# The small parts of 48 MLP weight chunks from an adding DMA, and 24 rounded parts from a casting DMA

## The chip, the cores and the metric

The kernel runs on one core of a Trainium2 chip. The metric is device time in microseconds. On the core, TensorE (PE in the profile) multiplies, VectorE (DVE) and ScalarE (ACT) work on whole tiles, GpSimd (POOL) does little here, and SyncE (SP) issues the weight loads. SP and POOL issue DMAs, which 16 DMA engines carry out for both.

## The reference: what is computed

One decoder layer on 256 tokens of width 2048 in float32: differential attention and a causal convolution module side by side, merged by gates, a projection, then an MLP of width 8192.

```python
m = jax.nn.sigmoid(zga) * attn_out + jax.nn.sigmoid(zgc) * conv_out
h = h + rms_norm(m @ w_out[l], post_mix_gain[l], NORM_EPS)
u = rms_norm(h, pre_ff_gain[l], NORM_EPS)
f = jnp.square(jax.nn.relu(u @ w_ff1[l])) @ w_ff2[l]
h = h + rms_norm(f, post_ff_gain[l], NORM_EPS)
```

All matrix products together read about 285 MB of weights once.

## The kernel before

**Weights as two parts.** TensorE multiplies in float32r, a rounded float32. To keep the precision, each weight w is split into wh, w rounded to float32r, and wl = w - wh; the activations likewise. Each product is then three: wh with the large and the small part of the activation, and wl with the large part.

**Chunks.** All weights come in 272 chunks of 128 x 2048 float32 (1 MiB), in the order in which they are multiplied (`order`, lines 66 to 77). The last 128 are the MLP's: four quarters q, each with 16 chunks of w_f1 (`ct` 0 to 15) and then 16 of w_f2 (four blocks `n` of four `kc`). A chunk of w_f1 is multiplied by `ws_k` (line 168 with wh, 512 columns; line 171 with wl, 256 columns; 16 of each), one of w_f2 by `as_part` (lines 194, 195 and 196, of which 195 reads wl; 24 matmuls of 512 columns in all).

**From the load to the matmul.** `fill` keeps up to three chunks alive (WBUFS = 3): there are three buffers each of raw, wh and wl. For a chunk, SP loads raw (line 97), ScalarE writes wh (`split_hi`, line 103), VectorE writes wl = raw - wh (`split_lo`, line 109). wh and wl of a chunk are free when TensorE has done with the chunk three before; raw is free when the subtraction three before has read it. `take` hands the chunk to TensorE and `done` lets the next fill begin.

**Order.** A scheduler that simulates the program sets the order of each engine's instructions, except for pinned ones at the beginning of the kernel and of the MLP; each engine then works through its own list in that order and waits at its head. In the MLP ScalarE and VectorE also take the results out of PSUM: lines 185, 186, 638, 640, 153 and 154 for w_f1 (sum, scale, squared ReLU, split of the activation), 648 or 650 for w_f2. POOL issues four DMAs in the whole kernel and none in the MLP but the first of its stretch (line 627, the last gain).

Of the kernel before, what the change touches and what calls it, by code (L numbers as in the profile page):

```python
# [13 lines left out]
AF = mybir.ActivationFunctionType  # L14
ALU = mybir.AluOpType
# [7 lines left out]
KT = D // P  # L23
# [5 lines left out]
CHUNK = 2048  # L29
NB = D // 512  # L30
# [22 lines left out]
def tile_layer(ctx, tc, x, vecs, lams, rope_t, subln, b_conv, post_mix, post_ff,  # L53
               w_q, w_k, w_v, w_cv, w_cg, w_ga, w_gc, w_co, w_o, w_f1, w_f2, out):
    nc = tc.nc
# [9 lines left out]
    order = []  # L65
# [6 lines left out]
    for w in (w_ga, w_gc, w_co, w_o):  # L72
        order += [w[n, kc] for n in range(NB) for kc in range(4)]
    n_mix = len(order)
    for q in range(NQ):
        order += [w_f1[q * KT + ct] for ct in range(KT)]
        order += [w_f2[n, q * 4 + kc] for n in range(NB) for kc in range(4)]
    queue = []
    state = {"next": 0, "live": 0}

# [2 lines left out]
    def load(pieces):  # L83
        i = state["next"]
        state["next"] += 1
        state["live"] += 1
        chunk = (rawp.tile([P, CHUNK], F32, name="raw"), whp.tile([P, CHUNK], F32R, name="wh"),
                 wlp.tile([P, CHUNK], F32R, name="wl"))
        for j in range(pieces):
            load_part(chunk, i, j, pieces)  # L90
        queue.append(chunk[1:])
        return chunk

    def load_part(chunk, i, j, pieces, pinned=False):
        w = CHUNK // pieces
        sl = slice(j * w, (j + 1) * w)
        a = nc.sync.dma_start(chunk[0][:, sl], order[i][:, sl])
        if pinned:
            pin(a)

    def split_hi(chunk, a, b, pinned=False):
        raw, wh, wl = chunk
        i = nc.scalar.copy(wh[:, a:b], raw[:, a:b])  # L103
        if pinned:
            pin(i)

    def split_lo(chunk, a, b, eng=None, pinned=False):
        raw, wh, wl = chunk
        i = (eng or nc.vector).tensor_sub(wl[:, a:b], raw[:, a:b], wh[:, a:b].bitcast(F32))  # L109
        if pinned:  # L110
            pin(i)

    def fill():
        while state["live"] < WBUFS and state["next"] < len(order):
            pieces = 4 if state["next"] in (n_mix, n_mix + 1, n_mix + 3) else 1
            chunk = load(pieces)
            w = CHUNK // pieces
            for j in range(pieces):
                split_hi(chunk, j * w, (j + 1) * w)
                split_lo(chunk, j * w, (j + 1) * w)  # L120

    def take():
        if not queue:
            fill()
        return queue.pop(0)

    def done(refill=True):
        state["live"] -= 1
        if refill:
            fill()  # L130
# [384 lines left out]
    for j in range(8):  # L515
# [3 lines left out]
        for i in range(2):  # L519
            ct = 2 * j + i  # L520
# [44 lines left out]
    for n in range(NB):  # L565
        ps = as_block(ma, apart=(n == NB - 1))
        ns = slice(n * 512, (n + 1) * 512)
        with tc.high_priority(offset=CHAIN if n == NB - 1 else 0):
            for t in range(NT):
                sq = fin2.tile([P, 512], F32, name="fsq")  # L570
                nc.scalar.activation(sq, ps[t], AF.Square, accum_out=yss[:, t, n:n + 1])
                if n == NB - 1:
                    nc.scalar.activation(r1[:, t:t + 1], yss[:, t, n:n + 1], AF.Sqrt, bias=ypre[:, t:t + 1],
                                         scale=1.0 / D)
# [57 lines left out]
    for q in range(NQ):  # L632
# [9 lines left out]
        for n in range(NB):  # L642
            ps = as_block(ga, stagger=(q == NQ - 1 and n == NB - 1), apart=(q == NQ - 1 and n == NB - 1))
            ns = slice(n * 512, (n + 1) * 512)
            for t in range(NT):
# [5 lines left out]
                if q == NQ - 1:  # L651
                    last = n == NB - 1
                    with tc.high_priority(offset=CHAIN if last else 0):
                        sq = fin2.tile([P, 512], F32, name="fsq")
                        nc.scalar.activation(sq, dst, AF.Square, accum_out=fss[:, t, n:n + 1])
                        if last:
                            nc.scalar.activation(r3[:, t:t + 1], fss[:, t, n:n + 1], AF.Sqrt, bias=fpre[:, t:t + 1],
                                                 scale=1.0 / D)
# [75 lines left out]
```

## Time and profile before

| | before |
|---|---|
| time, median of 2 runs | 1568.25 us (1568.21 to 1568.29) |
| span of the profiled execution | 1566.2 us |
| TensorE busy | 1548.6 us, 99% |
| VectorE busy | 1105.2 us, 71% |
| ScalarE busy | 710.6 us, 45% |
| weight load, 1 MiB, issue to landing (median) | 4.8 us |
| mean data rate over the span | 190 GB/s |

The runs lie 2.0 us above the span, which runs from the first to the last instruction. Busy shares are averages over the whole kernel; the change is in the MLP alone, which begins after 840 us. A matmul's busy time overlaps with that of the next, so the pace of TensorE is read from the starts.

### The profile page before, as it was taken

Reading aid. Unit: us, or ns where it says so; the run is one execution under the profiler, and the core shown is the slowest. Engines: PE = TensorE matmul, PEld = TensorE weight load, DVE = VectorE, ACT = ScalarE, POOL = GpSimd, SP = SyncE. Lnnn points to the kernel's source line nnn. Section 1 sums busy time; section 2 is a strip of 40 time slices with the busy share of each in tenths; the row PEclk is TensorE's granted clock in tenths of the full one; section 3 lists DMA queues with packets and bytes.
Section 4 is the critical chain, followed back from the end, with each engine's and each line's share of the span. In section 5 each row is a group of like instructions: output and inputs, shape, how many; then the busy total and the mean of one; then the engine's idle time right before and its main releaser. Section 6 shows DMA issues by size and latency. Waiting matters only on the chain.

```text
span 1566.2 us, 19217 instructions
## 1 busy us (share of the span) xinstructions
PE 1548.6 (99%) x7870; PEld 1316.3 (84%) x7870; DVE 1105.2 (71%) x1391; ACT 710.6 (45%) x749; POOL 15.8 (1%) x36
## 2 busy tenths in 40 slices
PE   8999999999999999999999999999999999999997
PEld 7888888888888888888887888888888888888886
DVE  5999999999999977856546765456644665456654
ACT  5444454646454546633435543344433443334442
POOL 3000000000000000000000000000000000000000
PEclk8999999999999999999999999999999999999999
DMA  6655555544555555555754655555555555555552
GB/s 226 231 189 190 191 191 184 184 174 177 173 177 179 198 188 188 209 190 184 266 192 143 233 192 192 188 188 189 188 190 192 186 186 191 200 193 182 188 199 83
DMA packets 45863, 296.85 MB, mean 190 GB/s; under 512 B 5072, under 2 KB 5200, under 8 KB 11216
## 3 DMA queue, kind: packets, MB, share of 16 engines
q1 hardware_dynamic: 45072, 290.39, 52.4%
q0 software_dynamic: 704, 5.24, 0.9%
q8 instruction: 61, 1.00, 0.2%
q14 instruction: 26, 0.21, 0.0%
HBM read 293.52 MB, written 2.10 MB: 189 GB/s over the span
## 4 chain that ended last, share of the span: by engine, by line
PE 98%; DVE 1%; DMA 1%; ACT 0%; SPq 0%; issue 0%; DVEq 0%; ACTq 0%
PE ps L168 30%; PE ps L196 16%; PE ps L194 16%; PE ps L195 16%; PE ps L171 15%; PE po L454 1%; DMA x_sb<-in_x_dram 1%; PE s L426 0%; PE aux L234 0%; PE aux L194 0%; PE aux L195 0%; PE aux L196 0%; DVE y_sb L669 0%; PE s L425 0%; PE aux L547 0%; SPq L260 0%
## 5 line engine op out<-in xcount | busy, mean ns | idle before, releaser
L109 DVE TENSOR_TENSOR wl<-raw,wh 128x2048 fp32r<-128x2048 f32 (+2 forms) x286 | 620.3, 2171 | 395.2 <-ACT wh L103 394.3
L103 ACT CAST wh<-raw 128x2048 fp32r<-128x2048 f32 (+1 forms) x293 | 522.9, 1789 | 731.2 <-issue 333.1
L168 PE MATMUL ps<-act,wh 128*128 128x512 f32 x2048 | 725.2, 399 | 1.4 <-DVE act L158 1.3
L171 PE MATMUL ps<-act,wl 128*128 128x256 f32 x2048 | 573.7, 281 | 0.0
L168 PEld LDWEIGHTS ps<-act,wh 128*128 128x128 f32 x2048 | 384.9, 188 | 91.3 <-DVE act L158 2.5
L171 PEld LDWEIGHTS ps<-act,wl 128*128 128x128 f32 x2048 | 387.0, 189 | 1.2
L196 PE MATMUL ps<-wh,act 128*128 128x512 f32 x624 | 243.8, 391 | 0.0
L194 PE MATMUL ps<-wh,act 128*128 128x512 f32 x624 | 243.8, 391 | 0.0
L195 PE MATMUL ps<-wl,act 128*128 128x512 f32 x624 | 243.4, 390 | 0.0
L374 DVE SCALAR_TENSOR_TENSOR y_all<-c,vec,y_all 128x256 f32<-128x256 f32 x480 | 209.4, 479 | 0.4
L194 PE MATMUL ps<-wh,g 128*128 128x512 f32 x496 | 193.0, 389 | 0.0
L195 PE MATMUL ps<-wl,g 128*128 128x512 f32 x496 | 193.0, 389 | 0.0
L196 PE MATMUL ps<-wh,g 128*128 128x512 f32 x496 | 193.0, 389 | 0.0
L196 PEld LDWEIGHTS ps<-wh,act 128*128 128x128 f32 x624 | 117.1, 188 | 24.2
L195 PEld LDWEIGHTS ps<-wl,act 128*128 128x128 f32 x624 | 117.2, 188 | 24.0
L194 PEld LDWEIGHTS ps<-wh,act 128*128 128x128 f32 x624 | 117.1, 188 | 23.9
L194 PEld LDWEIGHTS ps<-wh,g 128*128 128x128 f32 x496 | 93.1, 188 | 19.4
L196 PEld LDWEIGHTS ps<-wh,g 128*128 128x128 f32 x496 | 93.1, 188 | 19.3
L195 PEld LDWEIGHTS ps<-wl,g 128*128 128x128 f32 x496 | 93.1, 188 | 19.2
L186 DVE TENSOR_TENSOR z<-z,ps 128x512 f32<-128x512 f32 x64 | 43.5, 680 | 0.0
L185 ACT COPY z<-ps 128x512 f32<-128x512 f32 x64 | 36.9, 577 | 0.0
L650 DVE TENSOR_TENSOR y_sb<-ps,y_sb 128x512 f32<-128x512 f32 x23 | 14.9, 686 | 20.2 <-PE ps L196 20.2
(162 smaller groups left out, 634.8 us busy)
## 6 DMA issues: line engine op xcount, KB each, us to landing
raw<-in_w_f_dram SPq DMA_DIRECT2D x124, 1024.0 KB, 4.8
raw<-in_w_q_dram SPq DMA_DIRECT2D x16, 1024.0 KB, 4.8
raw<-in_w_k_dram SPq DMA_DIRECT2D x16, 1024.0 KB, 4.8
raw<-in_w_v_dram SPq DMA_DIRECT2D x16, 1024.0 KB, 4.8
raw<-in_w_ga_dram SPq DMA_DIRECT2D x16, 1024.0 KB, 4.9
raw<-in_w_gc_dram SPq DMA_DIRECT2D x16, 1024.0 KB, 4.8
raw<-in_w_co_dram SPq DMA_DIRECT2D x16, 1024.0 KB, 4.8
raw<-in_w_o_dram SPq DMA_DIRECT2D x16, 1024.0 KB, 4.8
```

Of the source, the lines that this page charges most:

```text
L103: i = nc.scalar.copy(wh[:, a:b], raw[:, a:b])
L109: i = (eng or nc.vector).tensor_sub(wl[:, a:b], raw[:, a:b], wh[:, a:b].bitcast(F32))
L168: a = nc.tensor.matmul(ps, wh[:, sl], acts.both(k), start=(k == 0), stop=False)
L171: b = nc.tensor.matmul(ps[:, S:], wl[:, sl], acts.hi(k), start=False, stop=(k == KT - 1))
L185: nc.scalar.copy(dst, ps[:, :, S:])
L186: nc.vector.tensor_tensor(dst, dst, ps[:, :, 0:S], op=ALU.add)
L194: nc.tensor.matmul(ps, acts.hi(k, a, b), wh[:, sl], start=(k == 0), stop=False)
L195: nc.tensor.matmul(ps, acts.hi(k, a, b), wl[:, sl], start=False, stop=False)
L196: nc.tensor.matmul(ps, acts.lo(k, a, b), wh[:, sl], start=False, stop=(k == KT - 1))
L374: i = nc.vector.scalar_tensor_tensor(y, c[:, j:j + S], vcol(ct, V_DW + j), y, op0=ALU.mult, op1=ALU.add)
L454: nc.tensor.matmul(po[:, t], aT[:, w, i * P:(i + 1) * P], v[:, u, j, vo:vo + VD], start=(n == 0), stop=(n == len(terms) - 1))
L650: nc.vector.tensor_tensor(dst, ps[t], dst, op=ALU.add)
```

## The change

For 72 of the MLP's 128 chunks a part comes in another way. `ways` says which.

- **"near" and "far"**, 48 chunks of w_f2: in quarters 0 and 2 all 16, in quarters 1 and 3 those with odd kc. ScalarE writes the negated rounding of raw into wl (line 130 of the changed kernel); a DMA of POOL's adds the weights onto wl (line 131), so that wl = w - wh with no VectorE. For even n ("near") it reads raw in SBUF, for odd n ("far") it reads the weights from HBM once more. ScalarE writes wh as before, by a second instruction.
- **"cast"**, 24 chunks of w_f1: odd ct of quarters 1, 2 and 3. A DMA of POOL's reads the weights from HBM and writes them rounded into wh (line 126); VectorE then subtracts as before. SP's load of raw stays for all chunks.

```diff
--- before.py
+++ after.py
@@ -72,9 +72,14 @@
     for w in (w_ga, w_gc, w_co, w_o):
         order += [w[n, kc] for n in range(NB) for kc in range(4)]
     n_mix = len(order)
+    ways = {}
     for q in range(NQ):
         order += [w_f1[q * KT + ct] for ct in range(KT)]
-        order += [w_f2[n, q * 4 + kc] for n in range(NB) for kc in range(4)]
+        if q > 0:
+            ways.update({len(order) - KT + ct: "cast" for ct in range(1, KT, 2)})
+        for n in range(NB):
+            ways.update({len(order) + kc: "far" if n % 2 else "near" for kc in range(4) if q % 2 == 0 or kc % 2})
+            order += [w_f2[n, q * 4 + kc] for kc in range(4)]
     queue = []
     state = {"next": 0, "live": 0}
 
@@ -113,8 +118,19 @@
     def fill():
         while state["live"] < WBUFS and state["next"] < len(order):
             pieces = 4 if state["next"] in (n_mix, n_mix + 1, n_mix + 3) else 1
+            i = state["next"]
             chunk = load(pieces)
             w = CHUNK // pieces
+            way = ways.get(i)
+            if way == "cast":
+                nc.gpsimd.dma_start(chunk[1], order[i])
+                split_lo(chunk, 0, CHUNK)
+                continue
+            if way is not None:
+                nc.scalar.activation(chunk[2], chunk[0], AF.Copy, scale=-1.0)
+                nc.gpsimd.dma_start(chunk[2], order[i] if way == "far" else chunk[0], accum_op=ALU.add)
+                split_hi(chunk, 0, CHUNK)
+                continue
             for j in range(pieces):
                 split_hi(chunk, j * w, (j + 1) * w)
                 split_lo(chunk, j * w, (j + 1) * w)
```

The scheduler puts the new instructions in place. On ScalarE, before, at quarter 0's first w_f2 blocks (wh and raw by buffer number, y_sb the MLP's sum, ps PSUM):

```order
L103 CAST wh_7678<-raw_7677 128x2048
L103 CAST wh_7708<-raw_7707 128x2048
L103 CAST wh_7738<-raw_7737 128x2048
L648 COPY y_sb_6246<-ps_7622 128x512 x2
L103 CAST wh_7771<-raw_7770 128x2048
L103 CAST wh_7801<-raw_7800 128x2048
L103 CAST wh_7831<-raw_7830 128x2048
L103 CAST wh_7861<-raw_7860 128x2048
```

Now, at the same place:

```order
L130 ACTIVATE wl_7683<-raw_7681 128x2048
L108 CAST wh_7682<-raw_7681 128x2048
L130 ACTIVATE wl_7714<-raw_7712 128x2048
L108 CAST wh_7713<-raw_7712 128x2048
L664 COPY y_sb_6246<-ps_7625 128x512 x2
L130 ACTIVATE wl_7745<-raw_7743 128x2048
L108 CAST wh_7744<-raw_7743 128x2048
L130 ACTIVATE wl_7779<-raw_7777 128x2048
L108 CAST wh_7778<-raw_7777 128x2048
L130 ACTIVATE wl_7810<-raw_7808 128x2048
L108 CAST wh_7809<-raw_7808 128x2048
L130 ACTIVATE wl_7841<-raw_7839 128x2048
```

Each chunk has two ScalarE instructions there in place of one, the negated rounding (ACTIVATE) ahead of wh's, and none is queued behind a DMA.

On POOL, before, all that stands between the convolution's memsets and the kernel's end:

```order
L387 MEMSET c 128x30 x5
L486 DMA bco<-in_b_conv_dram 128x2048
L556 DMA pmx<-in_post_mix_dram 128x2048
L559 DMA h_sb<-in_x_dram 128x2x2048
L627 DMA pmx<-in_post_ff_dram 128x2048
```

Now, from the last gain to the first casts:

```order
L643 DMA pmx<-in_post_ff_dram 128x2048
L131 DMA wl<-raw 128x2048 x4
L131 DMA wl<-in_w_f_dram 128x2048 x4
L131 DMA wl<-raw 128x2048 x4
L131 DMA wl<-in_w_f_dram 128x2048 x4
L126 DMA wh<-in_w_f_dram 128x2048 x8
```

Behind the last gain (line 643 now) POOL issues nothing but the new DMAs, 72 in all, in the order of the chunks; each waits at the head of the queue for its chunk's ScalarE instruction or buffer.

On TensorE, before, where a chunk of quarter 1's w_f1 (wh_8320) begins:

```order
L168 MATMUL ps_8372<-act_6802,wh_8320 128x512
L171 MATMUL ps_8372<-act_6802,wl_8321 128x256
L168 MATMUL ps_8372<-act_6802,wh_8320 128x512
L171 MATMUL ps_8372<-act_6802,wl_8321 128x256
L168 MATMUL ps_8372<-act_6819,wh_8320 128x512
```

Now, at the same place; wh_8336 is a casting chunk, wh_8374 the plain one after it:

```order
L184 MATMUL ps_8388<-act_6802,wh_8336 128x512
L184 MATMUL ps_8474<-act_6802,wh_8374 128x512
L187 MATMUL ps_8388<-act_6802,wl_8337 128x256
L184 MATMUL ps_8388<-act_6802,wh_8336 128x512
L187 MATMUL ps_8388<-act_6802,wl_8337 128x256
L184 MATMUL ps_8388<-act_6819,wh_8336 128x512
```

The first matmul of the next chunk stands ahead of the second matmul of this one. The like is found at about a dozen borders of chunks in the MLP; at two of them (the ends of quarters 0 and 2) 16 and 21 matmuls are drawn forward. The list of SP has the same order as before.

## Rows read from the trace of the kernel before

**Rows 1.** The page's part 1: busy us, share of the span, instructions.
```profile
span 1566.2 us, 19217 instructions
PE 1548.6 (99%) x7870; PEld 1316.3 (84%) x7870; DVE 1105.2 (71%) x1391; ACT 710.6 (45%) x749; POOL 15.8 (1%) x36
```

**Rows 2.** The page's part 4: the chain that ended last, by engine.
```profile
PE 98%; DVE 1%; DMA 1%; ACT 0%; SPq 0%; issue 0%; DVEq 0%; ACTq 0%
```

**Rows 3.** The chain in order of time: start us, us, what; its end.
```profile
1556.96 0.61 DVE y_sb L650
```

**Rows 4.** Waits, 850 to 1550 us: who waits for whom, total us, times, longest.
```profile
DVE wl L109 <- ACT wh L103: 280.2, 124, 3.4
ACT wh L103 <- issue: 189.8, 60, 3.3
ACT wh L103 <- PE ps L196: 173.2, 50, 3.5
```

**Rows 5.** Waits of SP's DMA queue, 850 to 1550 us.
```profile
SPq L97 <- DVE wl L109: 639.2, 123, 20.7
```

**Rows 6.** Busy us by stretch: PE, PEld, DVE, ACT, POOL, PEclk, DMA share, GB/s.
```profile
1300.00:1400.00 100.00, 100.00 (x469) 83.59 (x469) 50.62 (x31) 35.66 (x21) 0.00 (x0) 1.00 0.54 192
1400.00:1500.00 100.00, 100.00 (x530) 85.47 (x529) 61.56 (x52) 42.61 (x36) 0.00 (x0) 1.00 0.54 189
```

**Rows 7.** Timeline in quarter 0, w_f2: start us, us, engine, line, operation.
```profile
1002.39 0.39 PE L194 MATMUL ps<-wh,g 128*128 128x512 f32 x1
...
1002.59 1.91 ACT L103 CAST wh<-raw 128x2048 fp32r<-128x2048 f32 x1 [3.53 <-PE ps L196]
...
1004.40 1.06 ACT L648 COPY y_sb<-ps 128x512 f32<-128x512 f32 x2
...
1004.53 2.29 DVE L109 TENSOR_TENSOR wl<-raw,wh 128x2048 fp32r<-128x2048 f32 x1 [3.15 <-ACT wh L103]
...
1007.83 0.39 PE L194 MATMUL ps<-wh,g 128*128 128x512 f32 x1
```

**Rows 8.** Timeline of ScalarE in quarter 1's w_f1.
```profile
1035.52 1.91 ACT L103 CAST wh<-raw 128x2048 fp32r<-128x2048 f32 x1 [3.73 <-PE ps L168]
...
1058.18 1.91 ACT L103 CAST wh<-raw 128x2048 fp32r<-128x2048 f32 x1 [3.23 <-issue]
```

**Rows 9.** Timeline of TensorE where the MLP begins.
```profile
844.01 0.50 PE L168 MATMUL ps<-act,wh 128*128 128x512 f32 x1 [0.45 <-DVE act L158]
```

**Rows 10.** Timeline of POOL: its DMA issues.
```profile
764.72 0.53 POOL L556 DMA_DIRECT2D pmx<-in_post_mix_dram  x1 [238.36 <-ACT act L153]
765.24 0.71 POOL L559 DMA_DIRECT2D h_sb<-in_x_dram  x1
```

**Rows 11.** Busy us by stretch while POOL's 3 MiB and SP's loads move.
```profile
765.00:768.00 3.00, 3.00 (x15) 2.46 (x15) 0.67 (x2) 2.99 (x3) 0.95 (x2) 1.00 1.00 391
768.00:771.00 3.00, 3.00 (x15) 2.49 (x14) 2.29 (x1) 0.93 (x2) 0.00 (x0) 1.00 0.99 407
771.00:774.00 3.00, 3.00 (x15) 2.49 (x14) 1.83 (x1) 1.14 (x1) 0.00 (x0) 1.00 1.01 426
774.00:777.00 3.00, 3.00 (x15) 2.49 (x14) 0.47 (x1) 1.33 (x1) 0.00 (x0) 1.00 1.01 418
```

**Rows 12.** DMA issues: line, queue, count, KB each, median us to landing.
```profile
raw<-in_w_f_dram SPq DMA_DIRECT2D x124, 1024.0 KB, 4.8
...
h_sb<-in_x_dram POOLq DMA_DIRECT2D x1, 2048.0 KB, 14.0
...
bco<-in_b_conv_dram POOLq DMA_DIRECT2D x1, 1024.0 KB, 6.9
pmx<-in_post_mix_dram POOLq DMA_DIRECT2D x1, 1024.0 KB, 7.1
pmx<-in_post_ff_dram POOLq DMA_DIRECT2D x1, 1024.0 KB, 5.0
```

**Rows 13.** Busy us by stretch where POOL's last gain moves.
```profile
846.00:849.00 3.00, 2.94 (x20) 2.68 (x20) 2.67 (x7) 2.16 (x8) 0.00 (x0) 1.00 0.96 339
```

## Prediction

> **What bounds the kernel now.** I read the page's first part, then the chain, then the waits. TensorE is busy 1548.6 of 1566.2 us, VectorE 71%, ScalarE 45% [rows 1], and 98% of the chain that ended last is TensorE's [rows 2]. The change touches only the MLP, so what counts is the MLP. Between 850 and 1550 us the longest waits are VectorE waiting for ScalarE (280.2 us), ScalarE waiting for TensorE or for nothing that the profile shows [rows 4], and SP's queue waiting for VectorE (639.2 us) [rows 5]; TensorE stands in none of them. In two windows of 100 us TensorE is busy throughout, VectorE 50.62 and 61.56 us [rows 6]. So the subtractions that go are work of an engine that is half idle, beside one that never waits.
>
> TensorE's pace: a w_f2 chunk is 24 matmuls, and the row at 1002.39 and its like at 1007.83 are 24 apart: 5.44 us a chunk [rows 7]. For w_f1 the ScalarE rounding starts at 1035.52 and, four chunks on, at 1058.18: 5.66 us [rows 8]. 64 of each make 710 us. The MLP's matmuls start at 844.01 [rows 9] and the last VectorE pieces of the chain begin around 1557 [rows 3]; that leaves some microseconds at both ends that hold no subtraction the change takes away. **No gain worth a per cent is there to be had**; the question is only whether the new path delivers in time.
>
> **The time that a chunk has.** With three buffers, chunk c+3 is prepared while c+1 and c+2 are multiplied. The row of ScalarE shows it: the rounding starts at 1002.59, when TensorE has freed the buffer, ends at 1004.50; the subtraction runs 1004.53 to 1006.82 [rows 7]. The chunk is wanted two chunks after 1002.39, at 1013.27. So before, 6.45 us were left over. Now:
> - adding chunk (48): negated rounding, then the adding DMA may take from 1004.50 to 1013.27, **8.8 us** from issue to landing. wh's own rounding runs on ScalarE beside it.
> - casting chunk (24): 2 x 5.66 less the subtraction (2.29) and some 0.3 of hand-over: **8.7 us**.
>
> **Costs, part by part.** Removed: 48 subtractions of 2.29 us from VectorE (110 us) and 24 roundings of 1.91 from ScalarE (46 us): hidden before, worth 0. Added to ScalarE: 48 roundings of 1.91 (92 us; the trace has no Copy with a scale of this shape, I take the rounding's row). In a run of adding chunks ScalarE then has 3.8 us of every 5.44, plus 1.06 for two copies every fourth chunk [rows 7]: covered, 0. Issue on POOL took 0.53 to 0.71 us [rows 10], 72 of them, on an engine that has nothing else to do in the MLP: 0. At about a dozen places TensorE's new order draws one matmul of the next chunk forward (at two, 16 and 21). That asks for the next chunk's wh a chunk earlier; it is ready 1.9 or 3.8 us after its buffer is freed, under one chunk's 5.44: 0.
>
> The moved bytes are what is left. Every chunk still has its 1 MiB load by SP; 72 chunks get a second MiB by POOL. The room: when POOL moved 3 MiB beside the loads, the 16 DMA engines were full (share 0.99 to 1.01) and moved 391, 407, 426 and 418 GB/s, mean 410 [rows 11]. At that rate 1 MiB (1.049 MB) costs 2.56 us of all engines. TensorE didn't wait in it, and matmuls kept their pace, so contention with TensorE costs 0.
>
> *The casting DMA.* The trace has no cast. From below it is a plain MiB; from above, twice that. Fixed part: POOL's last gain, 1 MiB, landed after 5.0 us [rows 12], 2.4 more than its 2.56; it ran alone, as the 3 us in which it moved hold 3 x 339 GB/s = 1.02 MB [rows 13]. With one load between its packets: 2.4 + 2.56 + 2.56 = 7.5 us, under 8.7; the POOL MiBs beside loads landed in 6.9 and 7.1 [rows 12]. Twice: 10.1, late by 1.4. I take plain, 0: it reads and writes as many bytes as those rows. Throughput per pair of chunks: 3 x 2.56 = 7.7 of 11.3 us, free.
>
> *The adding DMA.* No row shows one. It has to read the source and the old wl and write wl. From below, one plain MiB; the nearest row above is POOL's 2 MiB, 14.0 us to landing, a part of it behind the MiB issued before it [rows 12]; three passes if each of the three streams costs one. I take **two passes, 5.12 us**, as a move's read and write already go together in one pass and one more read is what is added.
> - Quarters 0 and 2, all 16 w_f2 chunks each: load and add are 3 x 2.56 = 7.68 us of DMA per 5.44 us of TensorE. The DMA engines become the bound: 2.24 x 32 = **+72 us**. Landing (2.4 + 5.12 + 2.56 = 10.1) doesn't bind beyond it: with three buffers a chunk needs 5.44 + 1.9 + 10.1 + 0.2 = 17.6 us for three, less than 3 x 7.68 = 23.
> - Quarters 1 and 3, every second chunk: 4 x 2.56 = 10.2 of 10.9 us per pair fits. Landing is 10.1 against 8.8: late by 1.3. The chunk two before is late too, and its wait lengthens this chunk's window by the same, so each is late by half: 0.65 x 16 = **+10 us**.
>
> Sum: +82 us. Span 1566.2 and the runs' 1568.25 differ by 2.05 us around the span, which stays: 1568.25 + 82 = **1650 us**.
>
> A sentence that this sum does without: the Trainium skill ("Collectives: The Full Stack", Why ReduceScatter is half of AllGather) says that an add in the DMA path is slow not for the arithmetic but because it needs two source reads on the same read ring, and gives 62.28 against 32.35 GB/s, a factor of 1.93. No run here shows it yet; by that factor, as an estimate, the quarters 0 and 2 would cost 32 x (2.93 x 2.56 - 5.44), some 66 us, where a plain price from the row of a plain move would cost nothing.
>
> **Rivals.**
> 1. *The adds are hidden* (not slower). An add costs one pass: 5.12 us per 5.44, it fits, and landing at 7.5 is under 8.8. Time 1568, give or take 3. For it: the full 12 us at 410 GB/s did not stall TensorE [rows 11]. Against: those moves read one byte per byte written. It decides at 5.44 / 2.56 - 1 = 1.12 passes per add; up to there the sum is 0.
> 2. *The adds cost more*: three passes. Quarters 0 and 2: (10.24 - 5.44) x 32 = 154. Quarters 1 and 3: a pair needs 12.8 of 10.9, 1.9 x 16 = 31. Time 1753. More still if small pieces or the cast to fp32r slow the engines, as no row bounds that; with casts at two passes 0.7 x 24 = 17 more.
> 3. *Near adds starve the loads.* A near add reads raw, so SP's load into that buffer waits for its landing, where before it waited for VectorE [rows 5]. Load (4.8 [rows 12], say 7 when shared), rounding 1.9, add 10.1: 19 us a turn of three buffers, under the 23 that DMA throughput already takes in quarters 0 and 2, so it adds nothing there. It decides when load and add together pass 21 us; then +1 us per 3 us beyond for 24 chunks: 1655 to 1660.
> 4. *Faster.* Only if a late subtraction holds TensorE somewhere; no such wait in the MLP [rows 4]. At best 2 to 3 us at the ends of the MLP: 1565. Not more, as VectorE's late pieces there follow TensorE's last matmuls, not subtractions [rows 3].
>
> **Chances.** Forecast (add of 1.3 to 2.5 passes, rival 3 within it) 0.55, its own range 1590 to 1700; rival 1 0.25; rival 2 0.17; rival 4 0.03. Two per cent, about what a measurement of this kernel can tell from no change, is 31 us: below 1537 nothing leads, 0.01; within, rival 1, rival 4 and the cheapest end of the forecast, 0.28; above, 0.71. The range must take in rival 1 at 1566, and goes up to rival 2's three passes, 1750, leaving out its dearer half.
>
> **What would show it.** Right: TensorE waits on wl in the w_f2 parts of quarters 0 and 2, ended by a DMA of POOL's; DMA share there near 1.0; a w_f2 chunk near 7.7 us in quarters 0 and 2, near 6.1 for the added ones of 1 and 3, w_f1 unchanged at 5.66; POOL's adds landing after 10 us or more, casts after 7 to 8. Wrong: TensorE 98% busy as before (one pass), waits in the w_f1 parts (the cast is dear), or chunks of 10 us and more (three passes or small packets).

## The result and the profile after

The changed kernel takes 1675.46 us (median of two runs, 1669.17 and 1681.75), before 1568.25 us: a ratio of 1.068 with a 95% interval of 1.066 to 1.071. The prediction was 1650 (1566 to 1750), slower with a chance of 0.71. The profiled execution has a span of 1667.4 us, 101.2 more than before, and it is the 1669.17 run; the other ran 12.6 us longer without a profile, and what differs in it can't be read.

The page's parts 1 and 2 of the changed kernel (busy us, then tenths in 40 slices; PEclk is TensorE's granted clock):

```profile
span 1667.4 us, 19365 instructions
PE 1582.7 (95%) x7870; PEld 1331.5 (80%) x7870; DVE 995.4 (60%) x1343; ACT 752.9 (45%) x773; POOL 69.4 (4%) x108
...
PE   8999999999999999999999988999999978799996
...
DVE  5999999999999878565576300365225510046433
ACT  5444445554645456344464545223432344412452
POOL 3000000000000000000000111000000011100000
PEclk8999999999999999999999999999999999899998
DMA  6655554445455545556545899778886699976885
```

TensorE's share falls from 99% to 95% [rows 1], though its busy time rises by 34 us: the same matmuls took longer in the slices in which PEclk shows 9 or 8. VectorE gave up 110 us, as worked out ahead, and nothing came of it. The DMA row has its 9s in two places, the w_f2 parts of quarters 0 and 2; the w_f2 parts of quarters 1 and 3 show 8.

The chain that ended last, by engine (compare [rows 2], where TensorE had 98%), and the waits between 850 and 1660 us that TensorE and ScalarE have on DMAs (who waits for whom, total us, times, longest; compare [rows 4], which had no line of TensorE's):

```profile
PE 71%; DMA 15%; issue 9%; DVE 2%; ACT 1%; POOL 0%; SPq 0%; DVEq 0%; POOLq 0%; ACTq 0%
```

```profile
ACT wl L130 <- DMA raw<-in_w_f_dram: 86.5, 24, 6.8
...
PEld ps L211 <- DMA wl<-in_w_f_dram: 45.3, 19, 4.3
PE ps L211 <- DMA wl<-in_w_f_dram: 37.2, 16, 3.9
...
PE ps L211 <- DMA wl<-raw: 25.4, 12, 3.1
```

TensorE waits at line 211, the matmul that reads wl, for the adding DMAs. Where the time went is read from the first matmuls of each part. TensorE's timeline of before, then of after, at the ends of quarter 0's w_f2:

```profile
937.08 0.39 PE L194 MATMUL ps<-wh,g 128*128 128x512 f32 x1
...
1024.15 0.39 PE L168 MATMUL ps<-act,wh 128*128 128x512 f32 x1
```

```profile
937.19 0.39 PE L210 MATMUL ps<-wh,g 128*128 128x512 f32 x1
...
1058.83 0.39 PE L184 MATMUL ps<-act,wh 128*128 128x512 f32 x1
```

87.1 us before, 121.6 after, of which 2.8 are the 16 matmuls of w_f1 drawn forward: 118.8. Read in the same way, in us:

| part | before | after | more | predicted |
|---|---|---|---|---|
| w_f2, quarter 0 (16 adds) | 87.1 | 118.8 | 31.8 | 36 |
| w_f2, quarter 2 (16 adds) | 87.1 | 125.9 | 38.8 | 36 |
| w_f2, quarter 1 (8 adds) | 87.1 | 103.0 | 15.9 | 5 |
| w_f2, quarter 3 (8 adds) | 87.0 | 98.8 | 11.8 | 5 |
| w_f1, quarters 1 to 3 (24 casts) | 271.3 | 272.0 | 0.7 | 0 |
| after the last matmul | 9.6 | 11.8 | 2.2 | 0 |

The sum is 101.2, the whole difference of the spans. Two small rows need a word. In w_f1 TensorE waits 3.0 us in all for late parts, but over long stretches its pairs of matmuls start 0.347 us apart, before 0.353; 0.7 is the net of the two, and no run shows why the spacing changed. The 2.2 us at the end come from the last block's order: its two halves are done 2.7 us apart, before 5.0, so VectorE is still at the first when the second is ready. Each run below with whole adds, or copies in their place, in quarter 3 has them. A long stretch of quarter 0's w_f2 by the windows view (columns as in [rows 6]), the DMA queues in it (packets, MB, share of the 16 engines' time in the stretch; q0 has POOL's DMAs, q1 SP's loads) and the DMA issues of the page's part 6 (KB each, us to landing):

```profile
985.00:1045.00 60.00, 49.28 (x196) 38.23 (x194) 0.00 (x0) 32.07 (x21) 6.79 (x8) 0.94 1.03 280
```

```profile
q0 software_dynamic: 1183, 8.51, 68.6%
q1 hardware_dynamic: 1138, 8.27, 33.8%
```

```profile
raw<-in_w_f_dram SPq DMA_DIRECT2D x124, 1024.0 KB, 7.7
wl<-raw POOLq DMA_DIRECT2D x24, 1024.0 KB, 10.2
wl<-in_w_f_dram POOLq DMA_DIRECT2D x24, 1024.0 KB, 12.4
wh<-in_w_f_dram POOLq DMA_DIRECT2D x24, 1024.0 KB, 8.2
```

The 16 engines are full (1.03) at 280 GB/s, where a plain move filled them at 410 [rows 11]: bytes move slower because some of them are moved for an add. Here an add takes 5.07 us of all engines (68.6% of 60 us for 8.51 MB) and a load 2.57, together 7.64 for each chunk of 5.44 us of TensorE's. Over the whole run the loads land after 7.7 us, before 4.8 [rows 12].

**A term that the sum did not have.** TensorE's timeline at the first late add of quarter 1, and two windows at and behind it:

```profile
1150.57 0.39 PE L212 MATMUL ps<-wh,g 128*128 128x512 f32 x1
1150.79 0.39 PE L210 MATMUL ps<-wh,g 128*128 128x512 f32 x1
1154.23 0.80 PE L211 MATMUL ps<-wl,g 128*128 128x512 f32 x1 [3.05 <-DMA wl<-raw]
1154.82 0.63 PE L212 MATMUL ps<-wh,g 128*128 128x512 f32 x1
1155.25 0.63 PE L210 MATMUL ps<-wh,g 128*128 128x512 f32 x1
...
1159.94 0.53 PE L212 MATMUL ps<-wh,g 128*128 128x512 f32 x1
1160.31 0.40 PE L210 MATMUL ps<-wh,g 128*128 128x512 f32 x1
1160.54 0.40 PE L211 MATMUL ps<-wl,g 128*128 128x512 f32 x1
```

```profile
1154.00:1160.00 6.00, 5.77 (x14) 4.57 (x15) 0.69 (x1) 0.98 (x2) 0.00 (x0) 0.50 1.02 188
1160.00:1166.00 6.00, 6.00 (x27) 4.96 (x26) 0.47 (x1) 1.91 (x1) 0.00 (x0) 0.98 0.96 391
```

TensorE waits 3.05 us; then its matmuls start 0.43 us apart where they start 0.23 apart before the wait, for about 5.5 us, and in the window 1154 to 1160 the granted clock is 0.50, the lower of its two levels (1.2 of 2.4 GHz). 13 matmuls at 0.2 more are 2.6 us: the wait costs nearly as much again behind it. Not every wait has this behind it: after one of 1.78 us at 954.4 the granted clock is 0.57 from 955 to 959, after one of 3.41 us at 1591.9 it is 1.00 from 1591 to 1597. Counted from start to start over the changed kernel's w_f2 parts, the waits are 22.1, 9.5, 26.1 and 9.3 us in quarters 0 to 3, and the matmuls at the lower clock 9.0, 6.3, 12.0 and 2.2 more.

### The profile page after: what moved, and what is told of

Read it like the earlier page. It is cut to its first block, busy times and chain, and to the rows that moved or that the text cites. A ratio compares the mean times of both kernels' runs of the same rounds, so it can differ in the third digit from the quotient of the medians.

```text
span 1667.4 us, 19365 instructions
## 1 busy us (share of the span) xinstructions
PE 1582.7 (95%) x7870; PEld 1331.5 (80%) x7870; DVE 995.4 (60%) x1343; ACT 752.9 (45%) x773; POOL 69.4 (4%) x108
## 3 DMA queue, kind: packets, MB, share of 16 engines
q0 software_dynamic: 11072, 80.75, 19.7%
## 4 chain that ended last, share of the span: by engine, by line
PE 71%; DMA 15%; issue 9%; DVE 2%; ACT 1%; POOL 0%; SPq 0%; DVEq 0%; POOLq 0%; ACTq 0%
PE ps L184 25%; PE ps L187 13%; PE ps L211 10%; PE ps L212 10%; PE ps L210 10%; DMA wl<-in_w_f_dram 6%; DMA raw<-in_w_f_dram 5%; DMA wl<-raw 3%; DMA wh<-in_w_f_dram 1%; DVE wl L114 1%; PE po L470 1%; POOL wl L131 0%; DMA x_sb<-in_x_dram 0%; ACT wl L130 0%; ACT wh L108 0%
## 5 line engine op out<-in xcount | busy, mean ns | idle before, releaser
L114 DVE TENSOR_TENSOR wl<-raw,wh 128x2048 fp32r<-128x2048 f32 (+2 forms) x238 | 508.2, 2146 | 394.3 <-ACT wh L108 321.1
L108 ACT CAST wh<-raw 128x2048 fp32r<-128x2048 f32 (+1 forms) x269 | 475.9, 1773 | 525.4 <-PE ps L212 223.1
L211 PE MATMUL ps<-wl,g 128*128 128x512 f32 x496 | 208.2, 420 | 62.7 <-DMA wl<-in_w_f_dram 37.2
L212 PE MATMUL ps<-wh,g 128*128 128x512 f32 x496 | 203.5, 410 | 0.0
L210 PE MATMUL ps<-wh,g 128*128 128x512 f32 x496 | 202.3, 409 | 0.0
L211 PEld LDWEIGHTS ps<-wl,g 128*128 128x128 f32 x496 | 99.2, 200 | 97.2 <-DMA wl<-in_w_f_dram 45.3
L130 ACT ACTIVATE wl<-raw 128x2048 fp32r<-128x2048 f32 x48 | 91.9, 1914 | 137.9 <-DMA raw<-in_w_f_dram 86.5
L210 PEld LDWEIGHTS ps<-wh,g 128*128 128x128 f32 x496 | 99.3, 200 | 22.4
L212 PEld LDWEIGHTS ps<-wh,g 128*128 128x128 f32 x496 | 99.8, 201 | 20.5
L169 ACT CAST g<-gg 128x512 fp32r<-128x512 f32 x32 | 19.7, 617 | 120.9 <-DVE gg L656 120.9
```

Source lines behind the costliest of these rows:

```text
L130: nc.scalar.activation(chunk[2], chunk[0], AF.Copy, scale=-1.0)
L169: nc.scalar.copy(t[:, :, 0:S], src)
L210: nc.tensor.matmul(ps, acts.hi(k, a, b), wh[:, sl], start=(k == 0), stop=False)
L211: nc.tensor.matmul(ps, acts.hi(k, a, b), wl[:, sl], start=False, stop=False)
L212: nc.tensor.matmul(ps, acts.lo(k, a, b), wh[:, sl], start=False, stop=(k == KT - 1))
```

## Experiments

Theory A, the prediction's: an add costs the DMA engines two passes, so in quarters 0 and 2 the engines are the bound; in quarters 1 and 3 an add lands later than its window allows. The rivals are told with each run. All times are medians, the reference run of before is 1568.2 to 1568.5 us in each set.

### Each part of the change alone

Adds of quarters 0 and 2 alone:

```diff
-        if q > 0:
-            ways.update({len(order) - KT + ct: "cast" for ct in range(1, KT, 2)})
...
-            ways.update({len(order) + kc: "far" if n % 2 else "near" for kc in range(4) if q % 2 == 0 or kc % 2})
+            ways.update({len(order) + kc: "far" if n % 2 else "near" for kc in range(4) if q % 2 == 0})
```

> Only the 32 adds of quarters 0 and 2; quarters 1 and 3 and all casts as in the kernel before. Theory A (an add costs two passes, so load and add fill the 16 DMA engines): quarters 0 and 2 lose as much as in the changed kernel, 32 and 39 us by its trace, so 1568 + 70 = about 1638 us, DMA share near 1.0 there, chunks near 7.5 us. Rival B (the casts and the odd quarters bring the loss in, by POOL's queue still holding earlier DMAs when an add is due): under 1610 us.

Measured 1638.2 us, ratio 1.045 (1.043 to 1.046).

Adds of quarters 1 and 3 alone, the casts left out in the same way:

```diff
-            ways.update({len(order) + kc: "far" if n % 2 else "near" for kc in range(4) if q % 2 == 0 or kc % 2})
+            ways.update({len(order) + kc: "far" if n % 2 else "near" for kc in range(4) if q % 2 and kc % 2})
```

> Only the 16 adds of quarters 1 and 3 (odd kc); the rest as before. Theory A: the DMA engines have room (share about 0.8), what costs is landing after more than the 8.8 us window, plus TensorE's half clock for some us after each wait: 16 + 12 us by the changed kernel's trace, so about 1596 us, with 6 to 9 waits of 2 to 4 us. If the late adds came from the casts ahead of them, 1568 to 1575 us.

Measured 1599.7 us, ratio 1.020 (1.018 to 1.021), with eight waits of TensorE's, 1.2 to 3.9 us each.

Casts alone:

```diff
-            ways.update({len(order) + kc: "far" if n % 2 else "near" for kc in range(4) if q % 2 == 0 or kc % 2})
```

> Only the 24 casts, no add. Theory A: they land in 7.5 to 8.5 us, under the 8.7 us they have, and cost nothing: 1568 to 1570 us. Rival (a cast costs two passes, or VectorE's queue behind the waiting subtraction delays TensorE): 1580 us or more, with TensorE waiting for VectorE in the w_f1 parts.

Measured 1574.5 us (1568.0 to 1579.4 in ten runs), ratio 1.003 (1.002 to 1.005): neither the one nor the other, though TensorE does wait for VectorE's subtractions in w_f1, 6.2 us in 6 waits. The losses are 70, 31 and 6 us, 107 in all, as much as the whole change loses by its median (its two runs lie 6 us to either side): the parts add up as far as that can tell, and rival B of the first run falls.

The price of a pass can be taken from these runs. The queue of POOL's DMAs, q0, by the page's part 3 (packets, MB, share of the 16 engines' span): before (with the load queue, q1), the casts alone, the adds of the odd quarters alone, the changed kernel.

```profile
q1 hardware_dynamic: 45072, 290.39, 52.4%
q0 software_dynamic: 704, 5.24, 0.9%
```

```profile
q0 software_dynamic: 4160, 30.41, 5.2%
```

```profile
q0 software_dynamic: 3008, 22.02, 6.0%
```

```profile
q0 software_dynamic: 11072, 80.75, 19.7%
```

Before, POOL's four DMAs took 0.9% of 1566.2 us, 14.1 us of all engines. With casts 5.2% of 1574.5 = 81.9, so a cast takes (81.9 - 14.1) / 24 = 2.82 us. With odd adds 6.0% of 1598.6 = 95.9, so an add takes 81.8 / 16 = 5.1 us. In the changed kernel 19.7% of 1667.4 = 328.5; less 14.1 and 24 casts (67.7) that leaves 246.7 / 48 = 5.14 us. The two passes of the prediction were 5.12.

### The same DMAs without the addition

```diff
-                nc.gpsimd.dma_start(chunk[2], order[i] if way == "far" else chunk[0], accum_op=ALU.add)
+                nc.gpsimd.dma_start(chunk[2], order[i] if way == "far" else chunk[0])
```

> The changed kernel with its 48 adding DMAs turned into plain ones of the same bytes, source, queue and waits; it leaves the addition out, so wl holds the rounded weights and not the remainder. Theory A (the add's second read is the cost): load and copy take 5.12 us of 5.44, landing about 7.5 of 8.8 us: 1568 to 1580 us. Rival B (POOL's queue, the rounding in the DMA or the longer path is the cost, whatever the DMA does): 1640 us or more, as with the adds.

Measured 1592.6 us (1590.0 to 1598.6), ratio 1.016 (1.014 to 1.018). The queue's row:

```profile
q0 software_dynamic: 11072, 80.75, 13.6%
```

13.6% of 1590.9 = 216.4; less 14.1 and 67.7, a plain copy of the same bytes takes 134.6 / 48 = 2.80 us. So the addition alone makes 5.14 out of 2.80, a factor of 1.84, and 83 of the 107 us. The Trainium skill ("Collectives: The Full Stack", Why ReduceScatter is half of AllGather) measures 1.93 between a ring's copying and its adding and explains it by two source reads for an add. This case's 1.84, for adds into SBUF on one core, is near it; that the second read is the reason here is not shown by any run. But 24 us were left where I had expected 0 to 12. By this run's trace the w_f2 parts of quarters 0 and 2 lose 13 of them, the w_f1 parts with the casts 6, quarter 3's w_f2 3 and the end 2. In the dense parts load and copy did not take the 5.12 us that I had from the 410 GB/s: from 945 to 1025 us the engines are full (0.99) at 371 GB/s, and by the queues' shares of these 80 us a load takes 2.83 us and a copy 2.75, 5.58 of 5.44. That is 4.5 us in 32 chunks; TensorE's timeline has the 13 as seven waits, 9.3 us, and the lower clock behind some of them, 2.8. Why the engines, though full, move less than in the burst is not shown.

### Half the columns

The 48 adds cut to 1024 of the 2048 columns; VectorE subtracts the rest:

```diff
+                half = slice(0, CHUNK // 2)
-                nc.scalar.activation(chunk[2], chunk[0], AF.Copy, scale=-1.0)
-                nc.gpsimd.dma_start(chunk[2], order[i] if way == "far" else chunk[0], accum_op=ALU.add)
+                nc.scalar.activation(chunk[2][:, half], chunk[0][:, half], AF.Copy, scale=-1.0)
+                nc.gpsimd.dma_start(chunk[2][:, half], (order[i] if way == "far" else chunk[0])[:, half],
+                                    accum_op=ALU.add)
                 split_hi(chunk, 0, CHUNK)
+                split_lo(chunk, CHUNK // 2, CHUNK)
```

> The changed kernel with each of the 48 adds cut to the first 1024 of 2048 columns (negated rounding and adding DMA on that half, VectorE subtracts the other half); casts as in the changed kernel. From the runs so far an add takes 5.1 to 5.2 us of all 16 DMA engines and a load 2.96. Theory A (the engines' time decides): 2.96 + 2.6 = 5.6 us of 5.44 in quarters 0 and 2, so the loss falls to 5 to 10 us for the adds and 6 for the casts: 1575 to 1590 us. Rival B (the count of adds and their fixed latency decide): 1620 us or more.

Measured 1583.6 us, ratio 1.009 (1.007 to 1.011). As many adds, as many issues and ScalarE instructions, half the bytes: 15 us lost in place of 107. The bytes decide, not the count of adds. That half an add also lands sooner can't be told apart in this run; the next two show that in the dense quarters it is the engines' time.

### Near or far

All adds from SBUF, then all from HBM:

```diff
-            ways.update({len(order) + kc: "far" if n % 2 else "near" for kc in range(4) if q % 2 == 0 or kc % 2})
+            ways.update({len(order) + kc: "near" for kc in range(4) if q % 2 == 0 or kc % 2})
```

> All 48 adds read raw in SBUF, none HBM. Theory A (passes of the DMA engines, whatever their source): quarters 0 and 2 lose 32 to 39 us each as in the changed kernel; total 1660 to 1685 us. Rival C (a second read of HBM is what costs, since far adds land in 12.4 us and near ones in 10.2): quarters 0 and 2 lose under 25 each, total under 1650. Rival D (near adds hold raw and starve SP's loads): quarters 1 and 3 lose more than 16 and 12 us, with ScalarE waiting for loads there.

```diff
-            ways.update({len(order) + kc: "far" if n % 2 else "near" for kc in range(4) if q % 2 == 0 or kc % 2})
+            ways.update({len(order) + kc: "far" for kc in range(4) if q % 2 == 0 or kc % 2})
```

> All 48 adds read HBM, none raw. Theory A: quarters 0 and 2 as before, 32 to 39 us each; total 1660 to 1685 us. Rival C (HBM's second read costs): quarters 0 and 2 lose over 45 each, total over 1695. Rival D (near adds hold raw): quarters 1 and 3 lose clearly less than 16 and 12 us and ScalarE's negated rounding no longer waits for loads there.

All near 1692.7 us (1687.9 to 1695.8), all far 1670.5 us (1668.8 to 1672.5). Quarter 0's w_f2 and quarter 1's w_f1 together lose 39.5 and 34.9 us (30.6 in the changed kernel), quarter 1's w_f2 19.4 and 14.4 (15.9), quarter 3's 16.2 and 13.6 (11.8). Rival C falls: a second read of HBM is not what costs, since far adds alone are no dearer than near ones. Rival D is right in half: near adds are the dearer ones in all parts, and ScalarE's negated rounding waits for loads 118.5 us in all, with far adds not at all; but far adds lose 14 us in each odd quarter without it. In the dense quarters the difference is the engines' time: with all near adds, from 945.5 to 1050.5 us, an add takes 5.25 us of all engines and a load 2.77, and the 13 chunks follow at 8.08; with all far ones, from 956.2 to 1045.1, it is 5.04 and 2.60, and the 12 chunks follow at 7.41. The engines are full in both (1.01 and 1.03), so no held load leaves them idle there. Why a near add takes more of their time is not shown.

### One add in four

Near adds for kc 3 alone, in all quarters, no casts:

```diff
-        if q > 0:
-            ways.update({len(order) - KT + ct: "cast" for ct in range(1, KT, 2)})
...
-            ways.update({len(order) + kc: "far" if n % 2 else "near" for kc in range(4) if q % 2 == 0 or kc % 2})
+            ways.update({len(order) + 3: "near"})
```

> One add in four (kc 3 of every block in all four quarters, 16 near adds), no casts. Theory A: engines have room, an add with little beside it lands in about 8.7 us against a window of 8.8: under 10 us lost, 1568 to 1578 us; each wait longer than some 2 us brings TensorE's half clock with it. Rival (each add costs by itself, through POOL or ScalarE): 16 x 1.7 to 2 us as in the run of the odd quarters alone, about 1597 us.

Measured 1570.3 us, ratio 1.001 (1.000 to 1.002). TensorE has no wait in the MLP; the adds land in 6.9 us:

```profile
wl<-raw POOLq DMA_DIRECT2D x16, 1024.0 KB, 6.9
```

An add with engines to spare fits its window of 8.8 us. It costs by what it meets, not by itself; the 2 us that are lost are those at the end.

### Landing sooner

Each add of the odd quarters in two DMAs of half the columns; then each cast of the casts alone:

```diff
-                nc.gpsimd.dma_start(chunk[2], order[i] if way == "far" else chunk[0], accum_op=ALU.add)
+                for half in (slice(0, CHUNK // 2), slice(CHUNK // 2, CHUNK)):
+                    nc.gpsimd.dma_start(chunk[2][:, half], (order[i] if way == "far" else chunk[0])[:, half],
+                                        accum_op=ALU.add)
```

> The run of the odd quarters alone (16 adds, 1600 us) with each add issued as two DMAs, columns 0 to 1023 and 1024 to 2047. The engines' time stays, 5.1 us an add; what changes is when the halves are ready: the first some 2.5 us earlier, and the second is wanted only 1.4 us after the first (six matmuls of 0.227). Theory A (an add that lands 2 us too late, and TensorE's half clock behind the wait): the waits shrink from 2 to 4 us to about 1, most of the half clock goes: 1575 to 1587 us. Rival E (the DMA engines or SP's loads held up are the cost, not the landing of one add): 1595 to 1605 us.

```diff
-                nc.gpsimd.dma_start(chunk[1], order[i])
-                split_lo(chunk, 0, CHUNK)
+                for half in (0, CHUNK // 2):
+                    nc.gpsimd.dma_start(chunk[1][:, half:half + CHUNK // 2], order[i][:, half:half + CHUNK // 2])
+                for half in (0, CHUNK // 2):
+                    split_lo(chunk, half, half + CHUNK // 2)
```

> The run of the casts alone (1574.5 us) with each cast issued as two DMAs of half the columns and VectorE's subtraction cut in two behind them. Theory A (a cast lands in 7.5 to 9 us where 8.45 are to be had, and the subtraction of 2.3 us comes behind it): half the subtraction moves ahead of the second landing, some 1.1 us of window more, so the 6 us shrink to 0 to 3: 1568 to 1571.5 us. Rival (the loss is VectorE's order, the subtraction blocking what stands behind it): 1573 us or more.

The casts: 1567.3 us, ratio 0.999 (0.998 to 1.000), no wait of TensorE's left. Their 6 us were late landing, with a whole subtraction still to come behind it. VectorE's timeline of the casts alone shows a late one (start us, us, ..., idle before):

```profile
1062.40 4.49 DVE L113 TENSOR_TENSOR wl<-raw,wh 128x2048 fp32r<-128x2048 f32 x2 [4.65 <-DMA wh<-in_w_f_dram]
```

POOL had issued that cast at 1053.33 and it landed 9.0 us later; the first of the two subtractions in this line ended when TensorE was already waiting.

The adds: 1596.3 us, ratio 1.018 (1.016 to 1.020). Here theory A fails: 3 us came back of 31, not 13 to 25. With whole adds, ScalarE's timeline in quarter 1 shows what it had not reckoned with:

```profile
1119.74 1.91 ACT L128 ACTIVATE wl<-raw 128x2048 fp32r<-128x2048 f32 x1 [2.92 <-PE ps L209]
...
1127.53 1.91 ACT L106 CAST wh<-raw 128x2048 fp32r<-128x2048 f32 x1 [3.57 <-DMA raw<-in_w_f_dram]
1135.03 1.91 ACT L128 ACTIVATE wl<-raw 128x2048 fp32r<-128x2048 f32 x1 [5.59 <-DMA raw<-in_w_f_dram]
```

The negated rounding at 1135.03, ahead of the next add, starts 5.59 us late because its chunk has not been loaded. SP's queue names the cause (1100 to 1600 us, who waits for whom):

```profile
SPq L100 <- DMA wl<-raw: 95.8, 8, 13.7
```

A near add holds raw until it has landed, and SP's loads stand in one queue behind it. When it lands they come together, and the next add meets them. What the engines did between issue and landing, for two adds of this run (issued at 1164.01 and at 1137.24; queues as above, shares of that time):

```profile
q0 software_dynamic: 144, 1.05, 75.2%
q1 hardware_dynamic: 64, 0.39, 13.7%
```

```profile
q1 hardware_dynamic: 455, 3.33, 64.1%
q0 software_dynamic: 144, 1.05, 37.3%
```

Either add takes 5.1 to 5.2 us of the engines for its 1.05 MB. The first meets 0.39 MB of loads and lands after 6.9 us. The second comes just behind a near add that held raw until 1135.1; it meets 3.33 MB of loads, the engines are full (101%), and it lands after 13.7 us.

### The odd quarters without near adds

All 16 adds far, without casts, whole and then in the halves of the diff above:

```diff
-            ways.update({len(order) + kc: "far" if n % 2 else "near" for kc in range(4) if q % 2 == 0 or kc % 2})
+            ways.update({len(order) + kc: "far" for kc in range(4) if q % 2 and kc % 2})
```

> The run of the odd quarters alone (16 adds, 1600 us), all of them far, so that no add holds raw. Theory E (near adds hold raw, SP's loads start late, ScalarE's roundings after them, and with them the next add): SP no longer waits for an add, and of the 31 us most goes: 1575 to 1585 us. Theory A (the add itself lands too late for its window): 1592 to 1602 us, as the far-only run of the whole change lost 14 us in each odd quarter.

> As the odd quarters alone with far adds only, each add issued as two DMAs of half the columns. Splitting the near and far adds alike gave 1596 us, with SP still waiting for near adds. If late landing (A) is what is left once raw isn't held, the halves give 1.4 us of window or more back to each add and take the half clock away: 8 to 15 us under the run with whole far adds. If neither landing nor raw but the engines' time decides, the two are equal within 3 us.

Measured 1595.4 us (1589.5 to 1596.3) and 1591.0 us (1589.4 to 1593.5). SP waits for no add any more, and that brings only 4 us back, in theory A's range; the halves bring 4 more, between the two expectations of that run. TensorE's waits in the first of these, as far as profiled (its fastest run, 1589.5), are 13.5 us and the matmuls at the lower clock 5.5 more. The largest is at the first add of each odd quarter:

```profile
1124.83 0.80 PE L209 MATMUL ps<-wl,g 128*128 128x512 f32 x1 [4.44 <-DMA wl<-in_w_f_dram]
```

The first of quarter 1 lands 11.7 us after its issue, and the engines had little room then: they were 94% busy, with 1.93 MB of loads beside it. Where no near add holds the loads, adds meet loads all the same. So held loads (E) and late landing (A) are not two separate causes: in both, the loads that the engines move while an add is under way go with how late it lands. With them go the clock behind some of the waits and the 2.2 us at the end; how the odd quarters' 31 us divide between them is not settled.

## Why the prediction was right, and where not

- **The bound and the sign**: right. No gain was to be had from VectorE; TensorE waits at the matmuls that read wl, in the parts named.
- **Two passes per add**: right, 5.14 us against 5.12, and 5.07 in the dense stretch beside loads of 2.57, the forecast's pass of 2.56. Against the copy in its place (2.80) it is 1.84 passes. That one more read makes the second pass, the forecast's reason, is not shown.
- **Quarters 0 and 2, +72 us**: 70.6. The chunks take 7.43 and 7.87 us for the 7.68 forecast, with the DMA share at 1.03. Alone they lose 70 us. This is the mechanism, not luck: the pass, the number of passes and the full engines were each as forecast.
- **Quarters 1 and 3, +10 us**: mis-sized, 27.7 in the profile and 31 alone. The step that failed is the landing: one value of 10.1 us for all adds, a fixed part, two passes and one load between, so that each is late by 1.3 and costs half of that. The mean of the 16 was 10.3 us, but they spread from 6.9 to 12.7, with 0 to 2.9 MiB of loads in between, and an early one gives nothing back for a late one: eleven were over 8.8 us, by 27.4 in all. TensorE's waits came to 18.8 us, and the lower clock added 8.5 that no step had. That the clock falls after a wait was in my reach: in the kernel before, TensorE waits 3.74 us until 13.78, and from 13 to 23 us the granted clock is 0.50.
- **Rival 3, held loads**: put at 0 outside quarters 0 and 2. It is at work in the odd quarters, where the held loads come together and make the next add late; but all-far adds alone take only 4 us less than the mixed ones, as they meet loads too.
- **Casts, 0**: a net 0.7 in the changed kernel, 6 alone. Alone the landing was 8.0 us in the median, forecast 7.5, but spread to 11.5 against the forecast's window of 8.7; a median under the window is no cover.
- **Rival 1, hidden adds**: its point of decision (1.12 passes) rested on 2.56 us a MiB, from a burst. With copies of one pass the engines took 2.83 for a load and 2.75 for a copy, more than the 5.44 together, and the loss is 24 us, 6 of them the casts', not 0.
- **The half-dozen us that remain** between the sum by the profile and the median are the second run's, which was longer.

## What to carry over

Before an engine's work is handed to DMAs, add up the DMA engines' time per step from the queues' own rows, taken where the engines are full, an addition as two moves, and compare it with the step's time; half-idle VectorE is worth nothing beside a TensorE that never waits. Where the engines have room, compare landing with the window by its slow cases, not its median, and count what the DMA meets on the engines and what it holds while it runs: here raw, and with it the loads queued behind. Price TensorE's waits with the lower clock that can follow: here 67 us of waits in w_f2 brought 29.5 more.

## What the runs showed of the hardware

- An adding DMA of 1 MiB into SBUF took 5.0 to 5.3 us of all 16 engines where they were full, from HBM the lower and from SBUF the upper figure; a casting one 2.82 and a plain one on the same queue 2.80 over their runs, so the casting cost next to nothing.
- POOL needed 0.84 to 0.88 us to issue an add of 1 MiB, 0.53 to 0.56 for a cast, 0.53 for the plain copy in the add's place.
- With the engines full, an add and the loads slow each other: the loads land after 10.9 us in quarter 0's w_f2, 4.8 before (the median of the run). An add landed after 6.9 us beside 0.39 MB of loads and after 13.7 beside 3.33 MB.
